# Seven heads' squares summed by one stationary column of ones into a row, read back as a column; attention logits kept negated

## The chip, the cores and the metric

The kernel runs on one core of one Trainium2 chip. The metric is the device time of one execution in microseconds (us); lower is better. Engines are named as in the profile: PE (TensorE, with PEld for its weight loads), DVE (VectorE), ACT (ScalarE), POOL (GpSimd) and SP (SyncE, which here only issues transfers).

## What is computed

One decoder layer over a sequence of 512 tokens, model width 1024, in float32. The part that the change touches is the differential attention: 8 heads, two softmaxes per head, the second one subtracted with a factor, and an RMS norm over the 128 values that a head gives for a token.

```python
def one_block(args):
    ...
    bias = jnp.transpose(bias_tab[rel_bucket(rel)], (2, 0, 1))
    logits = jnp.einsum('bqhcd,bkhcd->bhcqk', q_blk, k).astype(jnp.float32) * scale
    logits = logits + bias[None, :, None]
    logits = jnp.where(rel >= 0, logits, -jnp.inf)
    p = jax.nn.softmax(logits, axis=-1)
    attn = p[:, :, 0] - lam * p[:, :, 1]
    return jnp.einsum('bhqk,bkhe->bqhe', attn.astype(v.dtype), v)

out = lax.map(one_block, (qb, jnp.arange(nb, dtype=jnp.int32)))
out = jnp.transpose(out, (1, 0, 2, 3, 4)).reshape(B, S, N_HEADS, V_DIM)
out = rmsnorm(out, subln_g) * (1.0 - lambda_init)
```

Beside it run a recurrent branch (RG-LRU) and, after the merge of both, an MLP with squared ReLU.

## The kernel before

**Matmuls.** Each operand of a large matmul is split into a high part (fp32r, a cast on ACT) and a low part (the rest, a subtraction on DVE). `split` does both, `mm3` multiplies high by high, high by low and low by high into the same bank. Weights come through SP as raw tiles of 512 KB (`wraw`, two buffers), are split into `whi` and `wlo`, and feed the projections; a new load starts when DVE has made the low part out of the old raw tile.

**Attention as a pipeline of steps.** `attention` runs 32 steps: step s is head h = s // 4, block of 128 queries i = s % 4. What belongs to a step is spread over the following ones by `at(step, function)`:

- step s: `logits` (PE, two banks c = 0 and 1, width up to 512), then `soft_a`. It adds the bias table `toep` to the logits and takes each row's maximum (one DVE instruction per c, the profile's CUSTOM_DVE_ANT_0, and a short read of its accumulator), negates both maxima in one more instruction (`nm`), and ACT takes the exponential of logit minus maximum with a running sum.
- step s+1: `soft_b` (DVE) joins both softmaxes into `pe`.
- step s+2: `turn` transposes `pe` on PE; ACT casts the high part, and `turn_low` (DVE) makes the low part `pt`.
- step s+3, for every second block: `av` multiplies by the values. After a head's last block `post_a` copies the output (`of`) and squares it (`osq`) on ACT.

**The norm of a head** follows, counted from the head's last block s: at s+4 `post_b` sums the squares over the 128 partitions. For each of four token blocks the squares are the stationary operand and a column `ones` (fp32) moves: one column comes out, tokens on partitions. DVE adds the epsilon term (`se`, `ms`), POOL raises it to -1/2 and writes it to DRAM (`rdram`). At s+5 `post_c` reads it back, broadcast to all partitions (`rb`, issued by POOL), and at s+7 `post_d` multiplies `of` by it and splits the product into `aT`, the input of the output projection.

**What sets the order.** DVE, ACT and POOL run their instructions in the order in which the program records them. Within a step that is the list `order`; between steps, `fill_in` records projection work of the next pair of heads (`qkv_pair`, or `gate` after the last pair) for a given amount of PE time. PE's matmuls and SP's transfers are recorded without such a chain, and the tile framework places them at build time; on the chip each queue then runs in its fixed order. The PSUM banks of attention come from a ring of five (`at`), those of the projections from a ring of three (`acc`).

The tile `sum` (128 x 1024) in the pool `stg` is used after attention, by `weight_sums`. The tiles `apart` (128 x 16) and `apart2` (128 x 32) are allocated and not used.

Of the kernel before, what the change touches and what calls it, by code (L numbers as in the profile page):

```python
# [13 lines left out]
F32 = mybir.dt.float32  # L14
F32R = mybir.dt.float32r
I32 = mybir.dt.int32
AF = mybir.ActivationFunctionType
ALU = mybir.AluOpType
# [3 lines left out]
P = 128  # L22
S = 512
DM = 1024
NT = S // P
KT = DM // P
NH = 8
# [12 lines left out]
def tile_block(ctx: ExitStack, tc: tile.TileContext, x, w_in, w_rga, w_rgx, w_pa, w_pr, w_o,  # L40
               w_up, w_dn, rel_bias, smalls, lamv, onehot, out):
    nc = tc.nc

    cp = ctx.enter_context(tc.tile_pool(name="cp", bufs=1))
    dp = ctx.enter_context(tc.tile_pool(name="dp", bufs=1, space=bass.MemoryType.DRAM))
    wp = ctx.enter_context(tc.tile_pool(name="wp", bufs=3))
    hp = ctx.enter_context(tc.tile_pool(name="hp", bufs=1))
    sm = ctx.enter_context(tc.tile_pool(name="sm", bufs=4))
    sm.tile([P, 16], F32, name="apart", bufs=1)
    es_ps = ExitStack()  # L50

    def psum_pool(name):
# [24 lines left out]
    V, A, G, T = InOrder(nc.vector), InOrder(nc.scalar), InOrder(nc.gpsimd), nc.tensor  # L77
# [65 lines left out]
    def split(hi, lo, src, scale=None):  # L143
        if scale is None:
            A.copy(hi, src)
            V.tensor_tensor(out=lo, in0=src, in1=hi.bitcast(F32), op=ALU.subtract)
        else:
            A.activation(hi, src, AF.Copy, scale=scale)
            V.scalar_tensor_tensor(out=lo, in0=src, scalar=scale, in1=hi.bitcast(F32), op0=ALU.mult, op1=ALU.subtract)
# [59 lines left out]
    make_identity(nc, ident)  # L209
    ones = cp.tile([P, 1], F32, name="ones")  # L210
    G.memset(ones, 1.0)
    mhalf = cp.tile([P, 16], F32, name="mhalf")
    G.memset(mhalf, -0.5)

# [65 lines left out]
    stg = es_act.enter_context(tc.tile_pool(name="stg", bufs=1, side="right"))  # L280
    summed = [{p: dp.tile([P, 1024], F32, name=f"up{n}{p}") for p in ("M5", "M7", "M6", "M4")} for n in range(2, 8, 2)]

    def weight_sums(behind):
        t = stg.tile([P, 1024], F32, name="sum")
        G.tensor_copy(t[:, :1], behind[:, :1])
        for n in range(2, 8, 2):
            for blocks in (((0, None), (1, "M5"), (3, "M6"), (2, "M4")), ((1, None), (3, "M7"))):
                for b, p in blocks:
                    if p:
                        G.dma_start(t, w_up[n, b], accum_op=ALU.add)  # L290
                        G.dma_start(summed[n // 2 - 1][p], t)
                    else:
                        G.dma_start(t, w_up[n, b])
# [17 lines left out]
    with tc.tile_pool(name="p1", bufs=1) as p1:  # L311
# [28 lines left out]
        ps = [[psum("at"), psum("at")] for z in range(2)]  # L340
        for k0, k1 in pieces:
# [8 lines left out]
            for k in range(k0, k1):  # L350
                sq = ssq if k == 0 else p1.tile([P, S], F32, tag="sq", name="sq", bufs=2)
# [22 lines left out]
        rb = p1.tile([P, S], F32, name="rb")  # L374
# [31 lines left out]
    tdram = dp.tile([NH, TW], F32, name="tdram")  # L406
    trep = [dp.tile([1, P * TW], F32, name=f"trep{h}", tag=f"trep{h}") for h in range(NH)]
    rdram = dp.tile([NH, S], F32, name="rdram")

    es_at = ExitStack()  # L410
    wk = es_at.enter_context(tc.tile_pool(name="wk", bufs=1, reuse_waits="tile"))
    t2 = {n: wk.tile([P, 2], F32, name=n) for n in ("ls", "le")}
    t8 = [wk.tile([P, KT], F32, name=n) for n in ("ab", "e", "den", "s", "s2", "po", "tmp", "mxl")]
    wk.tile([P, 32], F32, name="apart2")
    halves = slice(0, 64), slice(64, P)
    toep = {}

# [163 lines left out]
    def attention(fills, qks, vs, pads):  # L581
        st = {}
# [15 lines left out]
        def soft_a(s):  # L598
            h, i = place(s)
            n = P * (i + 1)  # L600
            lg = st[s]
            mx = sm.tile([P, 2], F32, tag="mx", name="mx")
            pe = [work("pe") for _ in range(2)]
            for c in range(2):
                V.tensor_tensor_reduce(out=pe[c][:, :n], in0=lg[c][:, :n], in1=toep[h][:, 384 - P * i:512], scale=1.0,
                                       scalar=-3e38, op0=ALU.add, op1=ALU.max, accum_out=mx[:, c:c + 1])
            nm = sm.tile([P, 2], F32, tag="nm", name="nm")
            V.tensor_scalar(out=nm, in0=mx, scalar1=-1.0, scalar2=None, op0=ALU.mult)
            if i == 0:
                st["sums", h] = sm.tile([P, 2, NT], F32, tag="sums", name="sums", bufs=3)  # L610
            sums = st["sums", h]
            for c in range(2):
                A.activation(pe[c][:, :n], pe[c][:, :n], AF.Exp, bias=nm[:, c:c + 1], accum_out=sums[:, c, i:i + 1])
            st[s] = pe

        def soft_b(s):
# [39 lines left out]
        def post_a(h):  # L656
# [4 lines left out]
            A.activation(sq, o, AF.Square)  # L661
            st["of", h] = of, sq

        def post_b(h):
            of, sq = st["of", h]
            ps = psum("at")
            for t in range(NT):
                T.matmul(ps[:, t:t + 1], sq[:, t * P:(t + 1) * P], ones, start=True, stop=True)  # L668
            s0 = st["sums", h][:, 0, :]
            se = sm.tile([P, NT], F32, tag="se", name="se", bufs=1)  # L670
            V.scalar_tensor_tensor(out=se, in0=s0, scalar=EPS, in1=s0, op0=ALU.mult, op1=ALU.mult)
            ms = sm.tile([P, NT], F32, tag="ms", name="ms")
            V.scalar_tensor_tensor(out=ms, in0=ps[:, :NT], scalar=1.0 / P, in1=se, op0=ALU.mult, op1=ALU.add)
            rs = sm.tile([P, NT], F32, tag="rs4", name="rs4")
            G.tensor_tensor(out=rs, in0=ms, in1=mhalf[:, :NT], op=ALU.pow)
            G.dma_start(rdram[h, :].rearrange("(p t) -> p t", p=P), rs)

        def post_c(h):
            rb_ = wk.tile([P, S], F32, tag="rb", name="rb")
            G.dma_start(rb_, rdram[h:h + 1, :].broadcast_to([P, S]))  # L680
            st["rb", h] = rb_

        def post_d(h):
            of = st["of", h][0]
# [7 lines left out]
        def at(step, f, *a):  # L692
            acts.setdefault(step, []).append((f, a))

        for s in range(NH * NT):
            h, i = place(s)
            at(s, logits, s)
            at(s, soft_a, s)
            at(s + 1, soft_b, s)
            at(s + 2, turn, s)  # L700
            at(s + 2, turn_low, s)
            if i % 2 == 1:
                at(s + 3, av, s)
            if i == 3:
                at(s + 3, post_a, h)
                at(s + 4, post_b, h)
                at(s + 5, post_c, h)
                at(s + 7, post_d, h)
        for h in range(2, NH):
            at(NT * h - 3, toep_in, h)  # L710
        order = [toep_in, post_c, post_b, av, post_a, turn, logits, soft_a, soft_b, post_d, turn_low]
        for step in sorted(acts):
            j = step // (2 * NT)
            if step >= 37:
# [642 lines left out]
    last_of_chunk, pe, queue, seq = {}, None, {}, []  # L1357
# [56 lines left out]
    for kind, a, p, pairs in steps:  # L1414
        o = kind, a, p
        if kind == "pl":
            oc, kc = int(p[1]) % 2, int(p[1]) // 2
            for half in range(2):
                pe = task("PE", 2.73, plain_go(o, half), (pe, lows[o]))
# [4 lines left out]
            if p == "b3":  # L1424
                pe = task("PE", 0.46, norm_go, (pe, norm_split))
                seq.append("norm")
                turn = task("DVE", dve(512), lambda: V.tensor_scalar(out=r2, in0=banks["norm"], scalar1=1.0 / DM, scalar2=EPS, op0=ALU.mult, op1=ALU.add), (pe,))
# [19 lines left out]
        for u in (slice(0, 1), slice(1, 2)) if split_y else (slice(0, 2),):  # L1447
            key = (*b, u.start) if split_y else b
            pe = bank_task(key, 2.73 * len(pairs) / 4 * (u.stop - u.start) / 2 + 0.17 * (fresh and o in STEADY and u.start == 0), product_go(o, pairs, u, fresh), [pe, *after], fresh)
# [103 lines left out]
    for n in range(TRIES):  # L1553
        at = rng.uniform(-20.0, best)
# [53 lines left out]
```

## Time and profile before

| | |
|---|---|
| median of 3 runs | 840.35 us (839.96 to 840.93) |
| the profiled execution's own time | 840.35 us |
| its span (first to last instruction) | 838.6 us |
| busy PE, DVE, ACT, POOL | 832.1, 654.8, 478.9, 104.0 us |
| granted TensorE clock | 1.00 |
| attention steps (exponentials of step 0 to 31) | 81.8 to 268.5 us |
| weight casts in 75 to 285 us | 25, of 1.04 us each |

A row of the timeline gives start, duration, engine, line, operation, the tiles written and read, shapes, a count, and in brackets the idle time before it with what ended it. Several equal instructions in a row are merged into one row with their count; its duration is then that of the whole group. Matmuls overlap in the pipeline, so the time that one takes is read from its start to the start of the next. A row of the windows gives, for a stretch of time, its length and the busy time with the count of instructions of PE, PEld, DVE, ACT and POOL, then the clock, the share of the transfer engines and GB/s. A row of the waits gives who waited for whom: microseconds in total, times, longest. SPq is SP's queue of transfers. A row of the transfers gives the issuing queue, the count, the size of one and the median time from issue to landing.

### The profile page before, as it was taken

How to read it: one execution, taken by the hardware profiler on the slowest of the kernel's cores; microseconds unless marked ns; L12 is line 12 of the kernel's file. 1: busy time of each engine (PE TensorE's matmuls, PEld its weight loads, DVE VectorE, ACT ScalarE, POOL GpSimd, SP SyncE). 2: the span in 40 equal slices, each digit the busy share in tenths (PEclk: the TensorE clock that was granted, in tenths of full speed). 3: DMA queues.
4: the chain of work that ended last, by engine and by line, in shares of the span. 5: the costliest groups of instructions: out<-in, count | busy, mean ns of one | idle time of the engine just before them, and what ended most of it. 6: DMA issues, size and time to landing. Idle time of an engine off the chain costs nothing.

```text
span 838.6 us, 14384 instructions
## 1 busy us (share of the span) xinstructions
PE 832.1 (99%) x5686; PEld 765.0 (91%) x5686; DVE 654.8 (78%) x1077; ACT 478.9 (57%) x753; POOL 104.0 (12%) x132
## 2 busy tenths in 40 slices
PE   9999999999999999999999999999999999999998
PEld 7899999999988887888888888899999999999998
DVE  6776788887877336879766767899989969977996
ACT  7445466555665334685763345774488448645851
POOL 0041231413201101111111000000000000000000
PEclk9999999999999999999999999999999999999999
DMA  6357332433322346667657662355655576556563
GB/s 202 124 153 217 91 110 66 103 123 91 88 77 76 88 138 196 195 189 209 182 170 179 197 253 76 101 151 145 209 151 151 151 256 170 144 164 200 151 168 110
DMA packets 41172, 126.10 MB, mean 150 GB/s; under 512 B 4992, under 2 KB 9800, under 8 KB 41104
## 3 DMA queue, kind: packets, MB, share of 16 engines
q1 hardware_dynamic: 31152, 92.65, 33.6%
q0 software_dynamic: 9952, 32.53, 18.1%
q8 instruction: 45, 0.74, 0.3%
q14 instruction: 23, 0.19, 0.1%
HBM read 102.05 MB, written 11.05 MB: 135 GB/s over the span
## 4 chain that ended last, share of the span: by engine, by line
PE 87%; DVE 5%; DMA 4%; ACT 2%; issue 1%; SPq 0%; ACTq 0%; DVEq 0%
PE acc L69 37%; PE acc L139 14%; PE acc L140 13%; PE acc L141 13%; DMA wraw<-in_w_in_dram 3%; PE at L595 2%; DVE wlo L69 2%; PE at L139 2%; PE at L141 2%; PE at L140 2%; PE at L631 1%; ACT whi L69 1%; PE at L529 1%; DVE pe L69 1%; PE at L668 1%
## 5 line engine op out<-in xcount | busy, mean ns | idle before, releaser
L69 ACT CAST whi<-raw 128x1024 fp32r<-128x1024 f32 x109 | 112.2, 1049 | 93.8 <-DVE raw L69 34.1
L69 DVE TENSOR_TENSOR wlo<-wraw,whi 128x1024 fp32r<-128x1024 f32 (+2 forms) x86 | 96.9, 1148 | 73.7 <-ACT whi L69 73.6
L69 PE MATMUL acc<-us,whi 128*128 128x256 f32 x900 | 153.8, 277 | 0.0
L69 PE MATMUL acc<-h,whi 128*128 128x256 f32 (+1 forms) x851 | 153.7, 285 | 0.0
L69 DVE TENSOR_TENSOR wlo<-raw,whi 128x1024 fp32r<-128x1024 f32 x109 | 131.0, 1218 | 21.0 <-ACT whi L69 20.9
L69 PEld LDWEIGHTS acc<-us,whi 128*128 128x128 f32 x900 | 135.8, 188 | 0.0
L69 PEld LDWEIGHTS acc<-h,whi 128*128 128x128 f32 x851 | 130.7, 188 | 2.6
L69 PE MATMUL acc<-us,wlo 128*128 128x256 f32 x448 | 123.8, 276 | 0.0
L69 PE MATMUL acc<-h,wlo 128*128 128x256 f32 (+1 forms) x424 | 120.6, 285 | 0.0
L69 ACT CAST whi<-wraw 128x1024 fp32r<-128x1024 f32 (+2 forms) x86 | 82.5, 982 | 47.1 <-DMA wraw<-in_w_in_dram 31.6
L139 PE MATMUL acc<-whi,hT 128*128 128x256 f32 x384 | 108.3, 282 | 0.0
L140 PE MATMUL acc<-wlo,hT 128*128 128x256 f32 x384 | 107.1, 279 | 0.2 <-DVE wlo L69 0.2
L69 PEld LDWEIGHTS acc<-us,wlo 128*128 128x128 f32 x448 | 84.1, 188 | 0.0
L139 PE MATMUL acc<-hT,whi 128*128 128x512 f32 x208 | 81.7, 393 | 0.0
L141 PE MATMUL acc<-hT,wlo 128*128 128x512 f32 x208 | 81.2, 390 | 0.0
L69 PEld LDWEIGHTS acc<-h,wlo 128*128 128x128 f32 x424 | 79.6, 188 | 1.3
L141 PE MATMUL acc<-whi,hT 128*128 128x256 f32 x288 | 80.1, 278 | 0.0
L69 ACT ACTIVATE pe<-pe,nm 128x128 f32<-128x128 f32 (+3 forms) x64 | 35.6, 558 | 66.0 <-DVE nm L69 66.0
L140 PEld LDWEIGHTS acc<-wlo,hT 128*128 128x128 f32 x384 | 72.4, 188 | 0.6 <-DVE wlo L69 0.4
L139 PEld LDWEIGHTS acc<-whi,hT 128*128 128x128 f32 x384 | 72.3, 188 | 0.5 <-issue 0.2
L69 POOL TENSOR_TENSOR rs<-ms,mhalf 128x8 f32<-128x8 f32 (+1 forms) x25 | 39.4, 1579 | 187.2 <-DVE ms L69 187.2
L69 POOL DMA_DIRECT2D raw<-raw x24 | 20.7, 863 | 325.7 <-DVE raw L69 117.2
(208 smaller groups left out, 1749.0 us busy)
## 6 DMA issues: line engine op xcount, KB each, us to landing
wraw<-in_w_in_dram SPq DMA_DIRECT2D x54, 512.0 KB, 3.5
raw<-in_w_dn_dram SPq DMA_DIRECT2D x32, 512.0 KB, 4.3
raw<-in_w_up_dram SPq DMA_DIRECT2D x29, 512.0 KB, 4.3
raw<-raw POOLq DMA_DIRECT2D x24, 512.0 KB, 4.6
sum<-in_w_up_dram POOLq DMA_DIRECT2D x18, 512.0 KB, 5.5
wraw<-in_w_pa_dram SPq DMA_DIRECT2D x8, 512.0 KB, 4.7
wraw<-in_w_pr_dram SPq DMA_DIRECT2D x8, 512.0 KB, 4.3
wraw<-in_w_o_dram SPq DMA_DIRECT2D x8, 512.0 KB, 4.2
```

The lines of the kernel that those rows point to most:

```text
L69: ins = f(*a, **k)
L139: T.matmul(o, l[0], r[0], start=first, stop=False)
L140: T.matmul(o, l[0], r[1], start=False, stop=False)
L141: T.matmul(o, l[1], r[0], start=False, stop=last)
L529: T.transpose(out=ps[:, t * P:(t + 1) * P], in_=qn[t // 2][:, c0:c0 + P], identity=ident)
L595: T.matmul(lg[c][:, :N], qT[:, c, i * P:(i + 1) * P], qk[h % 2, z][:, c, :N], start=z == 1, stop=z == 2)
L631: T.transpose(out=tp[:, b * P:(b + 1) * P], in_=st[s][:, b * P:(b + 1) * P], identity=ident)
L668: T.matmul(ps[:, t:t + 1], sq[:, t * P:(t + 1) * P], ones, start=True, stop=True)
```

## The change

Two things are changed.

**Sums of squares.** For heads 0 to 6 the squares are split in two fp32r parts (`post_p`, step s+3, into the tile `sum`). `post_b` (s+4) makes a column of ones the stationary operand and moves both parts, 512 tokens each, into one bank: a row of 512 sums on one partition. `post_e` copies the row to SBUF (ACT) and writes it to DRAM (`mdram`, a transfer issued by ACT). `post_l` (s+5) reads it back through SP as a column per token block (`few`, which the profile names apart2 or apart). `post_c` (s+6) now holds the epsilon term, the power and the store to `rdram`; `post_r` (s+7) reads the broadcast, for these heads through SP; `post_d` comes one step later, at s+8. Head 7 keeps the old form and its steps. In `order`, `post_b` moves from before `av` to behind `logits`.

**Negated logits.** `soft_a` lets the DVE instruction scale by -1 and take the minimum, so that the accumulator is the negated maximum at once; the exponential scales by -1. The separate negation of the maxima is gone, and `nm` has eight buffers.

```diff
-    sm.tile([P, 16], F32, name="apart", bufs=1)
+    ones_r = sm.tile([P, 16], F32R, name="apart", bufs=1)[:, :1]
...
+    G.memset(ones_r.bitcast(F32), 1.0)
...
-    wk.tile([P, 32], F32, name="apart2")
+    few = wk.tile([P, 2, 4, NT], F32, name="apart2")
...
-            mx = sm.tile([P, 2], F32, tag="mx", name="mx")
+            nm = sm.tile([P, 2], F32, tag="nm", name="nm", bufs=8)
...
-                V.tensor_tensor_reduce(out=pe[c][:, :n], in0=lg[c][:, :n], in1=toep[h][:, 384 - P * i:512], scale=1.0,
-                                       scalar=-3e38, op0=ALU.add, op1=ALU.max, accum_out=mx[:, c:c + 1])
-            nm = sm.tile([P, 2], F32, tag="nm", name="nm")
-            V.tensor_scalar(out=nm, in0=mx, scalar1=-1.0, scalar2=None, op0=ALU.mult)
+                V.tensor_tensor_reduce(out=pe[c][:, :n], in0=lg[c][:, :n], in1=toep[h][:, 384 - P * i:512], scale=-1.0,
+                                       scalar=3e38, op0=ALU.add, op1=ALU.min, accum_out=nm[:, c:c + 1])
...
-                A.activation(pe[c][:, :n], pe[c][:, :n], AF.Exp, bias=nm[:, c:c + 1], accum_out=sums[:, c, i:i + 1])
+                A.activation(pe[c][:, :n], pe[c][:, :n], AF.Exp, scale=-1.0, bias=nm[:, c:c + 1], accum_out=sums[:, c, i:i + 1])
...
+        def post_p(h):
+            if h == NH - 1:
+                return
+            of, sq = st["of", h]
+            both = stg.tile([P, 2, S], F32R, tag="sum", name="osr")
+            split(both[:, 0], both[:, 1], sq)
+            st["of", h] = of, both
+
         def post_b(h):
-            of, sq = st["of", h]
+            both = st["of", h][1]
             ps = psum("at")
-            for t in range(NT):
-                T.matmul(ps[:, t:t + 1], sq[:, t * P:(t + 1) * P], ones, start=True, stop=True)
-            s0 = st["sums", h][:, 0, :]
+            if h == NH - 1:
+                for t in range(NT):
+                    T.matmul(ps[:, t:t + 1], both[:, t * P:(t + 1) * P], ones, start=True, stop=True)
+                st["ms", h] = ps[:, :NT]
+                post_c(h)
+                return
+            for z in range(2):
+                T.matmul(ps[:1, :], ones_r, both[:, z], start=z == 0, stop=z == 1)
+            st["row", h] = ps
+
+        def post_e(h):
+            if h == NH - 1:
+                return
+            ps = st["row", h]
+            row = wk.tile([P, S], F32, tag="osq", name="row")[:1, :]
+            A.copy(row, ps[:1, :])
+            A.dma_start(mdram[h:h + 1, :], row)
+
+        def post_l(h):
+            ms = st["ms", h] = few[:, h % 2, 0, :]
+            nc.sync.dma_start(ms, mdram[h, :].rearrange("(t p) -> p t", p=P))
+
+        def post_c(h):
+            s0, got = st["sums", h][:, 0, :], st["ms", h]
...
-            V.scalar_tensor_tensor(out=ms, in0=ps[:, :NT], scalar=1.0 / P, in1=se, op0=ALU.mult, op1=ALU.add)
+            V.scalar_tensor_tensor(out=ms, in0=got, scalar=1.0 / P, in1=se, op0=ALU.mult, op1=ALU.add)
...
-        def post_c(h):
-            rb_ = wk.tile([P, S], F32, tag="rb", name="rb")
-            G.dma_start(rb_, rdram[h:h + 1, :].broadcast_to([P, S]))
-            st["rb", h] = rb_
+        def post_r(h):
+            rb_ = st["rb", h] = wk.tile([P, S], F32, tag="rb", name="rb")
+            (G if h == NH - 1 else nc.sync).dma_start(rb_, rdram[h:h + 1, :].broadcast_to([P, S]))
...
                 at(s + 3, post_a, h)
+                at(s + 3, post_p, h)
                 at(s + 4, post_b, h)
-                at(s + 5, post_c, h)
-                at(s + 7, post_d, h)
+                at(s + 4, post_e, h)
+                if h < NH - 1:
+                    at(s + 5, post_l, h)
+                    at(s + 6, post_c, h)
+                    at(s + 7, post_r, h)
+                    at(s + 8, post_d, h)
+                else:
+                    at(s + 5, post_r, h)
+                    at(s + 7, post_d, h)
...
-        order = [toep_in, post_c, post_b, av, post_a, turn, logits, soft_a, soft_b, post_d, turn_low]
+        order = [toep_in, post_l, post_c, post_r, av, post_a, turn, logits, post_b, soft_a, soft_b, post_p, post_e, post_d, turn_low]
```

How this moves instructions is shown at three places, all around head 0's sum of squares. PE first, before the change: ten rows of one step behind the last product with the values. `acc` are projections, `ones,osq` is the sum of squares.

```order
L595 MATMUL at<-kl_487,qkT 128x384
L139 MATMUL acc<-whi,hT 128x256
L140 MATMUL acc<-wlo,hT 128x256
L141 MATMUL acc<-whi,tail 128x256
L139 MATMUL acc<-whi,hT 128x256
L140 MATMUL acc<-wlo,hT 128x256
L141 MATMUL acc<-whi,tail 128x256
L139 MATMUL acc<-whi,hT 128x256
L668 MATMUL at<-ones,osq 128x1 x4
L140 MATMUL acc<-wlo,hT 128x256
```

The sum stands 7 projection matmuls behind the logits of step 6; another 20 projection matmuls follow, and then the transposes (`ident,pe`) and the logits of step 7. PE after the change, at the end of the same stretch (`osr,apart` are the two new matmuls, apart being the ones):

```order
L139 MATMUL acc<-whi,hT 128x256
L631 MATMUL at<-ident,pe 128x128 x2
L597 MATMUL at<-qkT 128x512
L597 MATMUL at<-kl_489,qkT 128x512
L597 MATMUL at<-qkT 128x512
L597 MATMUL at<-kl_489,qkT 128x512
L682 MATMUL at<-osr,apart 1x512 x2
L140 MATMUL acc<-wlo,hT 128x256
```

Between the logits of step 6 and the transposes there are now 26 projection matmuls and no sum of squares; the sum stands behind the logits of step 7. In heads 2 and 4 the new order has the same 26.

DVE in step 6 before the change (ISA rows are the addition with row maximum and the read of its accumulator; `wlo` are weights):

```order
L69 ISA pe,mx<-at,toep 128x384
L69 ISA mx 128x1
L69 ISA pe,mx<-at,toep 128x384
L69 ISA mx 128x1
L69 TENSOR_SCALAR nm<-mx 128x2
L69 RECIPROCAL rc<-sums 128x1
L69 SCALAR_TENSOR_TENSOR r_1428<-sums,lneg,rc 128x1
L69 SCALAR_TENSOR_TENSOR pe<-pe,r_1428 128x256
L69 TENSOR_TENSOR pt_496<-at,pt_495 128x128
```

And after it:

```order
L69 ISA pe,nm<-at,toep 128x384
L69 ISA nm 128x1
L69 ISA pe,nm<-at,toep 128x384
L69 ISA nm 128x1
L69 RECIPROCAL rc<-sums 128x1
L69 SCALAR_TENSOR_TENSOR r_1416<-sums,lneg,rc 128x1
L69 SCALAR_TENSOR_TENSOR pe<-pe,r_1416 128x256
L69 TENSOR_TENSOR osr<-osq,osr 128x512
L69 TENSOR_TENSOR pt_498<-at,pt_497 128x128
```

The negation is gone, and the low part of the squares stands between `pe` and the low part of the transposed block. `se` and `ms`, which stood in step 7, stand in step 9, ahead of its two additions; `ms` there reads the column.

ACT after the change, steps 6 and 7 of the same head (`whi` are weights, `v` the values, `qkT` queries):

```order
L69 COPY of<-at 128x512
L69 ACTIVATE osq<-at 128x512
L69 CAST pt_497<-at 128x128
L69 ACTIVATE pe,sums<-pe,nm 128x384 x2
L69 CAST osr<-osq 128x512
L69 CAST whi<-wraw 128x1024 x2
L69 CAST v<-acc 128x512
L69 CAST pt_497<-at 128x2x128
L69 ACTIVATE pe,sums<-pe,nm 128x512 x2
L69 COPY row<-at 1x512
L69 DMA mdram<-row 1x512
L69 ACTIVATE qkT<-at,qg 64x512 x2
```

The rows osr, row and mdram are new; the others stood in this order before. Each of the two exponentials of a step now waits for its own accumulator read, where before the first waited for the negation of both.

On SP, each of the seven heads adds a read of the column and a read of the broadcast between the weight loads; on POOL seven of the eight broadcast reads are gone.

More of the change, by code (lines that the diff above doesn't have):

```diff
@@ L283, in weight_sums @@
     def weight_sums(behind):
-        t = stg.tile([P, 1024], F32, name="sum")
+        t = stg.tile([P, 1024], F32, tag="sum", name="sum")
         G.tensor_copy(t[:, :1], behind[:, :1])
@@ L408, in tile_block @@
     rdram = dp.tile([NH, S], F32, name="rdram")
+    mdram = dp.tile([NH, S], F32, name="mdram")
     es_at = ExitStack()
```

## Prediction

> **What bounds the kernel now.** I read the page first, then the windows, then what TensorE (PE) waits for, then single rows in order of time.
>
> ```profile
> span 838.6 us, 14384 instructions
> ...
> PE 832.1 (99%) x5686; PEld 765.0 (91%) x5686; DVE 654.8 (78%) x1077; ACT 478.9 (57%) x753; POOL 104.0 (12%) x132
> ```
>
> PE shows 99%, but a busy PE need not be a fast one. So here is a stretch of the attention part, 75 to 295 us, and every wait of PE in it:
>
> ```profile
> 200.00:220.00 20.00, 19.68 (x161) 18.99 (x161) 16.68 (x47) 13.02 (x30) 6.61 (x8) 1.00 0.31 82
> ...
> PE at L631 <- DVE pe L69: 0.3, 1, 0.3
> ...
> PEld at L631 <- issue: 1.0, 3, 0.4
> PEld at L631 <- DVE pe L69: 0.6, 3, 0.2
> ```
>
> The granted clock is 1.00. DVE (VectorE) has 3.3 us of 20 left in that stretch, ACT 7. In 220 us PE itself waits once, for 0.3 us, and its weight loads for a few tenths each. The attention part is therefore bound by PE's instruction stream: what is taken out of that stream shortens the span, as long as no other engine is then late. What stands behind attention is PE work too, so a gain there is not waited away later.
>
> **What the change takes from PE.** Today each head's squares cost eight PE passes (four matmuls of one column in fp32, two passes each). Head 4 and head 0:
>
> ```profile
> 214.02 0.28 PE L141 MATMUL acc<-whi,tail 128*128 128x256 f32 x1
> 214.14 0.95 PE L668 MATMUL at<-ones,osq 128*128 128x1 f32 x8
> 214.94 0.36 PE L139 MATMUL acc<-whi,hT 128*128 128x256 f32 x1
> 215.14 0.28 PE L140 MATMUL acc<-wlo,hT 128*128 128x256 f32 x1
> ...
> 114.20 0.28 PE L139 MATMUL acc<-whi,hT 128*128 128x256 f32 x1
> 114.49 1.05 PE L668 MATMUL at<-ones,osq 128*128 128x1 f32 x8
> 115.40 0.36 PE L140 MATMUL acc<-wlo,hT 128*128 128x256 f32 x1
> 115.60 0.28 PE L141 MATMUL acc<-whi,hT 128*128 128x256 f32 x1
> ```
>
> I go by starts, since durations of pipelined matmuls overlap. A 256-column matmul takes 0.12 (214.02 to 214.14). From 214.14 to 215.14 are 1.00 us, of which one such matmul is 0.12: the group costs 0.88, its slow change back to the other kind of matmul included. In head 0, which also waits for the squares, 114.20 to 115.60 less two matmuls is 1.16. Six heads at 0.88 and head 0 at 1.16 make 6.4 us.
>
> In their place come two fp32r matmuls of 512 columns for each of the seven heads, with one stationary column. The nearest rows are the MLP norm's pair, also ones against 512 fp32r columns, but with 128 stationary columns, and a matmul with few stationary columns, in fp32:
>
> ```profile
> 55.25 1.26 PE L452 MATMUL at<-oh,rbt 64*32 64x512 f32 x4
> ...
> 546.61 0.62 PE L69 MATMUL acc<-s,h 128*128 128x512 f32 x2
> 547.07 0.39 PE L69 MATMUL acc<-h,whi 128*128 128x256 f32 x2
> ```
>
> The norm's pair takes 0.46 (546.61 to 547.07). The other row moves 2 x (512+128) = 1280 columns in 1.26, or 1.0 us for 2 x 512. I take 0.46, because type and size are those of the norm's pair; the ends are 0.46 and 1.0. Seven pairs are 3.2 us, so PE's stream gets **3.2 us shorter** (6.4 - 3.2). The Trainium skill, "TensorE: Matmul & The Clock Gate", section "Back-to-back issue gap", makes the time one of moving columns alone (N/2.4 + 2.5 ns): two at 512 would be an estimated 0.43, and seven 3.0. No row here shows it for one stationary column.
>
> **What PE then waits for.** The removed group stood in front of the next pair of transposes and of the logits of the step after; the new pair stands behind those logits. So PE reaches both sooner, and their inputs must be ready sooner. Head 0:
>
> ```profile
> 113.50 0.28 PE L139 MATMUL acc<-whi,hT 128*128 128x256 f32 x1
> ...
> 117.76 0.38 PE L631 MATMUL at<-ident,pe 128*128 128x128 f32 x2
> ...
> 118.91 0.28 PE L139 MATMUL acc<-whi,hT 128*128 128x256 f32 x1
> ...
> 115.38 0.08 DVE L69 DVE_READ_ACCUMULATOR2_ANT mx<- 128x1 f32 x1
> ...
> 115.97 0.17 DVE L69 TENSOR_SCALAR nm<-mx 128x2 f32<-128x2 f32 x1
> 116.05 0.15 DVE L69 RECIPROCAL rc<-sums 128x1 f32<-128x1 f32 x1
> ...
> 116.50 0.48 DVE L69 SCALAR_TENSOR_TENSOR pe<-pe,r 128x256 f32<-128x256 f32 x1
> ...
> 116.18 0.62 ACT L69 ACTIVATE pe<-pe,nm 128x384 f32<-128x384 f32 x1 [1.59 <-DVE nm L69]
> ...
> 117.39 1.98 ACT L69 CAST whi<-wraw 128x1024 fp32r<-128x1024 f32 x2
> ```
>
> The new order has 26 projection matmuls between the logits and the transposes: from 113.50 at 0.114 each PE arrives at 116.46 instead of 117.76. What it transposes, pe, is finished at 116.98, or 116.90 without the negation (only 0.08 later than nm does rc start). PE waits 0.45 there. From the transposes to the end of the logits are 1.15 us (117.76 to 118.91), so the new pair is reached at 118.05.
>
> Is its input there by then? The negation goes, and with it the one wait of both exponentials on nm: each waits only for its own row minimum. The first may start once the first read is done, 115.46 and a hop of 0.04 (nm ends at 116.14, the exponential starts at 116.18), so at 115.50. Both take 1.21 (116.18 to 117.39), so ACT is free for the new cast at 116.71, and DVE's subtraction follows it:
>
> ```profile
> L69 ACT CAST s<-scratch x1: 622/622/622, 532.0 to 532.0; 128x512 fp32r<-128x512 f32 x1
> L69 DVE TENSOR_TENSOR s<-scratch,s x1: 684/684/684, 533.0 to 533.0; 128x512 fp32r<-128x512 f32 x1
> ```
>
> 116.71 + 0.62 + 0.68 = 118.01. The first matmul needs only the cast half, the second starts 0.23 later: no second wait. With the exponentials where they are today the cast would start at 117.39 and the subtraction end at 118.69, a further 0.4 behind the second matmul's 118.28.
>
> Heads 2 and 4 stand in the same order, 26 matmuls, so I count 0.45 three times: **1.4 us back**. In heads 1, 3, 5 and 6 more work lies between the logits and the new pair, or the pe in question is ready sooner; I take nothing, and keep 0 to 0.45 for each.
>
> **What is added beside PE.** DVE loses 32 negations at 0.08 and gains seven subtractions at 0.68: 4.8 against 2.6, and while it waits for the cast it does nothing. The product with rb and the second subtraction of each head move one step later, out of the step that gets the new one, so that step is no longer than today. ACT gains the cast (0.62), the row's copy and a DMA issue per head (rows of 0.59 and 0.38 stand further down), into its waits:
>
> ```profile
> ACT pe L69 <- DVE nm L69: 66.0, 29, 3.7
> ...
> SPq L103 <- DVE wlo L69: 148.0, 22, 17.2
> ```
>
> 66 us of ACT's idle time cover seven times about 1.6. The 14 transfers that SP's queue gets stand among weight loads that wait 148 us for raw buffers already; in this part ACT has no wait for a weight, so a few microseconds of delay there cost nothing. Without that cover each would push back a cast and what follows on ACT. POOL loses seven issues; it is 12% busy. I put these together at -0.2: the existing waits for pe shrink a little. Range -0.8 to +1.
>
> **Sum**: -3.2 + 1.4 - 0.2 = -2.0 us. The profiled execution took 840.35 with a span of 838.6 (1.75 lies around it), and 840.35 is the median of the runs too. Forecast: span 836.6, time **838.3**.
>
> **Rivals.** *DVE takes it back.* DVE has 3.3 us of 20 left. If heads 1, 3 and 5 wait 0.45 as well, another 1.35 goes and the time is 839.7; with the second wait of 0.4 in three heads, 840.9. For it: heads 0 to 5 run in the same dense part. Against: DVE's own list does not get longer in the crowded step.
>
> *One stationary column is no cheaper than the row with 32.* At 1.0 a pair, seven cost 7.0: -3.2 becomes +0.6, and the sum 842.1. Against: that row is fp32.
>
> *The column comes late, and the kernel is slower.* The sum now goes PSUM, row, DRAM, column, and DVE's ms waits for it in order. Decisive is head 6, where the low half of the last transposed block stands behind ms, and the last product of attention (av) behind that:
>
> ```profile
> 268.37 0.18 ACT L69 ACTIVATION_READ_ACCUMULATOR pe<-pe,nm 128x1 f32 x1
> ...
> 274.79 0.69 DVE L69 TENSOR_TENSOR pt<-at,pt 128x512 fp32r<-128x512 f32 x1
> ...
> 278.41 0.59 ACT L69 COPY of<-at 128x512 f32<-128x512 f32 x1 [3.65 <-PE at L141]
> ...
> 0.74 0.38 SPq L325
> ...
> rdram<-rs POOLq DMA_DIRECT2D x8, 2.0 KB, 2.3
> ...
> rbt<-in_rel_bias_dram SPq DMA_DIRECT2D x1, 1.0 KB, 3.2
> ...
> xT<-in_x_dram SPq DMA_DIRECT2D x3, 512.0 KB, 7.3
> ```
>
> From the exponentials (268.55, or 0.7 sooner, 267.85): copy 0.59, issue 0.38, landing 2.3, issue 0.38, so the read starts at 271.5. It must be in by 274.7 to change nothing: 3.2 us. Those products end at 278.4 and take twelve matmuls, 1.4, so they begin at 277.0 and there is about 1.5 more before PE waits: it decides from a read of **4.7 us** on. No row shows a read of 512 single elements; the nearest by size take 2.3 to 3.2, the slowest of all 7.3. I take 3.2. At 7.3 head 6 costs 2.6. Heads 1, 3 and 5, with shorter steps, I estimate at 1 each, so 5.6 in all: 843.9, slower. The Trainium skill speaks against the change here: "DMA: Bandwidth & Descriptors", section "Rules for kernel authors", says that a last dimension that isn't contiguous becomes one descriptor per element, here 512 of 4 bytes. By that rule the late case comes true if such descriptors run much slower than the 16-byte pieces of rdram<-rs, whose 128 landed in 2.3.
>
> *It gains more.* With no wait at the transposes and fewer of today's: -3.2 - 1.2, so 836.0.
>
> **How the numbers follow.** Forecast 0.50 (its own range 837.0 to 839.6), DVE takes it back 0.22, the column late 0.12, the dear column 0.06, more gain 0.10. The range 836.2 to 842.1 leaves out most of the late column and half of the larger gain. Some 0.2%, or 1.7 us, is what a measurement of this kernel tells from no change. Faster by more than that: the larger gain and 0.43 of the forecast, 0.53. Within: the rest of the forecast and nearly all of the give-back, 0.30. Slower: the late column, most of the dear one, 0.17.
>
> **What would show it.** The new pair's starts 0.23 apart, and 0.46 to the next matmul; exponentials that start 0.65 sooner after their logits; PE waits of 0.3 to 0.6 before the two transposes of heads 0, 2 and 4, on DVE's pe; no DVE wait before ms of over 1 us, and none of PE before the last av. I am wrong if the pair takes 1.0, if PE waits for osr, or if DVE stands at ms for several microseconds.

## The result, and the profile after

The changed kernel takes **837.9 us** (median of 22 runs, 835.85 to 840.8) against 840.2 for the kernel before (22 runs): ratio 0.9972, 95% interval 0.9963 to 0.9981. The forecast was 838.3. The time came out as predicted, but by luck: two errors cancel, as the experiments show. The execution that was profiled took 836.11 us, 1.8 below its own median, so differences in its trace are read by mechanism and not added up to the result.

The page of the changed kernel, span and busy time:

```profile
span 834.3 us, 14347 instructions
...
PE 828.1 (99%) x5644; PEld 759.1 (91%) x5644; DVE 654.2 (78%) x1052; ACT 486.0 (58%) x767; POOL 99.8 (12%) x126
```

PE has 42 matmul records fewer (seven times eight passes against two). DVE is as busy as before, because the subtractions (7 x 0.69) cost about what the negations saved (32 x 0.17); ACT has 7 us more.

Now step 6 of the changed kernel, the part in which head 0's squares are prepared (timeline, rows of ACT, DVE and PE):

```profile
113.35 0.56 DVE L69 CUSTOM_DVE_ANT_0 pe<-at,toep 128x384 f32<-128x384 f32 x1
...
113.97 0.62 ACT L69 ACTIVATE pe<-pe,nm 128x384 f32<-128x384 f32 x1
...
114.76 0.48 DVE L69 SCALAR_TENSOR_TENSOR pe<-pe,r 128x256 f32<-128x256 f32 x1
...
115.18 0.60 ACT L69 CAST osr<-osq 128x512 fp32r<-128x512 f32 x1
...
115.82 0.69 DVE L69 TENSOR_TENSOR osr<-osq,osr 128x512 fp32r<-128x512 f32 x1 [0.58 <-ACT osr L69]
115.82 0.38 PE L631 MATMUL at<-ident,pe 128*128 128x128 f32 x2
...
116.97 0.62 PE L682 MATMUL at<-osr,apart 128*1 128x512 f32 x2
117.43 0.28 PE L140 MATMUL acc<-wlo,hT 128*128 128x256 f32 x1
```

The pair costs 0.46 (116.97 to 117.43), as forecast. Here `pe` is ready at 115.24, and the transposes at 115.82 wait for nothing. DVE stands 0.58 for the cast of the squares.

Without the negation two things come sooner, counted from the step's first reduction. In the kernel before, that reduction started here:

```profile
114.89 0.56 DVE L69 CUSTOM_DVE_ANT_0 pe<-at,toep 128x384 f32<-128x384 f32 x1
```

With the two rows of step 6 in the prediction, the first exponential started 1.29 later (116.18), and now 0.62; DVE's own join, which writes the `pe` that PE transposes, started 1.61 later (116.50), and now 1.41. The join comes some 0.2 sooner in most of the 32 steps.

What PE and its weight loads wait for from 75 to 295 us in the changed kernel (us in total, times, longest):

```profile
PE at L631 <- DVE pe L69: 0.4, 2, 0.2
PE acc L141 <- DVE wlo L69: 0.3, 1, 0.3
...
PEld at L631 <- DVE pe L69: 1.3, 4, 0.4
PEld acc L141 <- DVE wlo L69: 0.7, 1, 0.7
PEld at L139 <- ACT pt L69: 0.7, 3, 0.3
PEld at L631 <- issue: 0.6, 3, 0.3
PEld at L597 <- issue: 0.5, 2, 0.3
PEld at L631 <- ACT pe L69: 0.5, 2, 0.2
PEld acc L139 <- issue: 0.5, 3, 0.2
```

With two more rows of 0.2 these are 5.9 us. The same list of the kernel before has, beside the three rows that the prediction shows, these five, and adds up to 3.8:

```profile
PEld at L139 <- ACT pt L69: 0.5, 2, 0.3
PEld at L529 <- DVE qn L69: 0.5, 2, 0.3
PEld at L595 <- issue: 0.5, 2, 0.3
PEld at L668 <- ACT osq L69: 0.2, 1, 0.2
PEld at L140 <- DVE pt L69: 0.2, 1, 0.2
```

None of these rows is large, but their sum matters for this case: 3.8 before, 5.9 after, and from 0.2 to 22.3 in the experiments below. A held-up load and the matmul behind it both have rows, so the sum is not exact. Nor does it rank kernels with different streams: the changed kernel waits more than the kernel before and is faster.

### The profile page after: what moved, and what is told of

Read it like the earlier page. It is cut to its first block, busy times and chain, and to the rows that moved or that the text cites. A ratio compares the mean times of both kernels' runs of the same rounds, so it can differ in the third digit from the quotient of the medians.

```text
span 834.3 us, 14347 instructions
## 1 busy us (share of the span) xinstructions
PE 828.1 (99%) x5644; PEld 759.1 (91%) x5644; DVE 654.2 (78%) x1052; ACT 486.0 (58%) x767; POOL 99.8 (12%) x126
## 2 busy tenths in 40 slices
DMA packets 45329, 126.11 MB, mean 151 GB/s; under 512 B 8695, under 2 KB 13503, under 8 KB 45262
## 4 chain that ended last, share of the span: by engine, by line
PE 90%; DVE 4%; ACT 2%; DMA 2%; issue 1%; SPq 0%; POOL 0%; DVEq 0%; ACTq 0%; POOLq 0%
PE acc L69 37%; PE acc L141 15%; PE acc L140 15%; PE acc L139 15%; PE at L597 2%; PE at L139 2%; PE at L141 2%; PE at L140 2%; DVE wlo L69 2%; PE at L631 1%; DMA wraw<-in_w_in_dram 1%; PE at L531 1%; DVE pe L69 1%; ACT pe L69 0%; DVE xT L69 0%
## 5 line engine op out<-in xcount | busy, mean ns | idle before, releaser
L69 ACT CAST whi<-wraw 128x1024 fp32r<-128x1024 f32 (+2 forms) x86 | 82.6, 982 | 43.7 <-DMA wraw<-in_w_in_dram 29.2
L139 PE MATMUL acc<-hT,whi 128*128 128x512 f32 x208 | 81.5, 392 | 0.0
L69 ACT ACTIVATE pe<-pe,nm 128x128 f32<-128x128 f32 (+3 forms) x64 | 35.6, 559 | 43.9 <-DVE nm L69 43.7
L140 PE MATMUL acc<-hT,whi 128*128 128x512 f32 x156 | 60.8, 390 | 0.0
```

Of the source, the lines that this page charges most:

```text
L69: ins = f(*a, **k)
L139: T.matmul(o, l[0], r[0], start=first, stop=False)
L140: T.matmul(o, l[0], r[1], start=False, stop=False)
```

## The experiments

### The two edits apart

**Only the negated logits**, on the kernel before:

```diff
-            mx = sm.tile([P, 2], F32, tag="mx", name="mx")
+            nm = sm.tile([P, 2], F32, tag="nm", name="nm", bufs=8)
...
-                                       scalar=-3e38, op0=ALU.add, op1=ALU.max, accum_out=mx[:, c:c + 1])
-            nm = sm.tile([P, 2], F32, tag="nm", name="nm")
-            V.tensor_scalar(out=nm, in0=mx, scalar1=-1.0, scalar2=None, op0=ALU.mult)
+                                       scalar=3e38, op0=ALU.add, op1=ALU.min, accum_out=nm[:, c:c + 1])
...
-                A.activation(pe[c][:, :n], pe[c][:, :n], AF.Exp, bias=nm[:, c:c + 1], accum_out=sums[:, c, i:i + 1])
+                A.activation(pe[c][:, :n], pe[c][:, :n], AF.Exp, scale=-1.0, bias=nm[:, c:c + 1], accum_out=sums[:, c, i:i + 1])
```

> The kernel before with only the logits' edit: the reduction writes the negated logits and their minimum, the exponential takes scale -1, the 32 negations of the maximum on DVE are gone; the squares are summed as before. Theory (the gain of 2.3 us is the shorter matmul stream, PE being the bound): 839.5 to 840.2 us, ratio 0.9993 to 1.0000, because each exponential starts some 0.6 us sooner but PE waits for none of them. Rival (the sooner exponentials are the gain): 838 us, ratio 0.997. In the trace the first waits for nm on ACT should shrink in both cases (ACT's pe <- DVE nm summed 66.0 us over 29 waits before and 43.7 over 26 after, from 75 to 295 us).

Measured: 837.23 us, ratio 0.9963 (0.9949 to 0.9977). My theory fell. The negation alone gives as much as the whole change.

**Only the new sums**: the changed kernel with the old maximum and its negation put back (the same lines the other way round).

> The changed kernel with the logits' edit undone: maximum of the plain logits, then a negation of its own on DVE; the sums of squares, their row, the way through DRAM and the order as after. Theory: the stream is 3.1 us shorter as after, but the exponentials start some 0.6 us later, so osr's low half comes up to 0.4 us late at the pair in heads 0, 2 and 4 and the transposes' waits grow: 838.2 to 839.4 us, ratio 0.9976 to 0.9990. Rival (the gain needs the negation): 840 us or more. Second rival (the negation is without any effect): 837.9, ratio 0.9972.

Measured: 847.34 us, ratio 1.0083 (1.0062 to 1.0104), 7 us slower than before and far behind the theory (838.2 to 839.4); the first rival, 840 or more, came true. The sums, meant to relieve PE, are a loss by themselves.

**Only the place of the sum**, behind the logits, on the kernel before:

```diff
-        order = [toep_in, post_c, post_b, av, post_a, turn, logits, soft_a, soft_b, post_d, turn_low]
+        order = [toep_in, post_c, av, post_a, turn, logits, post_b, soft_a, soft_b, post_d, turn_low]
```

> The kernel before with one name moved in the order of a step: the sums of squares (the old four matmuls of plain float32 with a column of ones, and the two small DVE operations behind them) stand behind the logits rather than ahead of them. Theory (order matters only by what PE waits for, and PE waited for nothing there): 839.9 to 840.6 us, ratio 0.9995 to 1.0005. Rival (the place behind the logits is a gain of its own, since the logits and so the exponentials start 0.88 us sooner): 839 us or less. Other rival (DVE stands at ms for the later sums and holds up the softmax behind it): 841 or more.

Measured: 840.49 us, ratio 1.0001 (0.9985 to 1.0017), as the theory had it.

**No return through DRAM**, the changed kernel without these two transfers:

```diff
-            A.dma_start(mdram[h:h + 1, :], row)
...
-            nc.sync.dma_start(ms, mdram[h, :].rearrange("(t p) -> p t", p=P))
```

> The changed kernel without the two transfers of the return: the row is still copied out of PSUM, but it isn't written to DRAM and no column is read; the mean squares of seven heads are taken as 1.0 from a tile set once, so the computation leaves out that the sums reach the normalisation. Theory (the column lay ready 2.4 to 7 us ahead of its use, the issues stand on queues off the path): 837.7 to 838.2 us, the time after, ratio to before 0.9969 to 0.9976. Rival (the return costs something by ACT's issues of 0.2 us or the 512 packets of 4 bytes): 836.5 to 837.3.

Measured: 840.27 us, ratio 0.9999 (0.9986 to 1.0011): less work, and 2.4 us slower than the changed kernel. No theory had that. Its waits name something the missing transfers have no part in, the low part of the transposed block ahead of `av`:

```profile
PE at L140 <- DVE pt L69: 1.9, 4, 0.7
...
PEld at L140 <- DVE pt L69: 2.9, 4, 0.9
```

The order of its matmuls, in turn, differs from the changed kernel's: by the names of their operands, 442 of the 5644 PE instructions in the two traces differ from those at the same place. The framework places PE's matmuls and SP's transfers at build time, and any edit makes it place them anew. So an edit and the order that it happens to get had to be separated.

### The same edits with PE's order held

The next kernels record each matmul and each transfer of SP and tie it to the one ahead of it in a given list, so that both queues run in an order chosen by me:

```diff
+    for u, v in zip(place_PE, place_PE[1:]):
+        tc.add_manual_dep(issued['PE'][v], issued['PE'][u].name, ORDER, reason="order")
```

and the same for SP. The added recorder has line 90, which the profile then shows for every matmul. The traces have PE's instructions in exactly the given order. The complete changed kernel was not run with its own order held; the nearest to it is the kernel without the return, below.

**Negated logits, in the order of the kernel before:**

> The kernel before with only the logits negated, but its matmuls and SP's transfers held in the order in which they stand in the kernel before (each depends on the one ahead of it, so the builder cannot place them anew). Two theories for the 3.1 us that the negation alone gained in the free build (837.23 against 840.31): A, the builder's new order of the matmuls (51 starts that are 60 to 120 ns late between 75 and 345 us where before has 74, since the sums of squares now stand beside the transposes; 6.6 to 4.5 us), with which the time here stays at 839.3 to 840.3; B, the exponentials that start sooner on the chip, with which it is 837.0 to 838.3 here too.

Measured: 836.99 us, ratio 0.9953 (0.9936 to 0.9970). Theory B: the gain is on the chip and not in the placing. Of all the waits of PE and its loads from 75 to 295 us one row is left:

```profile
PEld at L90 <- ACT osq L69: 0.2, 1, 0.2
```

3.8 us became 0.2: without the negation PE waits for almost nothing. Whether the sooner exponentials do that, as the expectation has it, or DVE's sooner join is not shown, since the edit brings both. One row of the kernel before, in the same stretch, speaks for the join: the join of a step (it begins with `rc`) had to wait for exponentials once, for 0.3.

```profile
DVE rc L69 <- ACT pe L69: 0.3, 1, 0.3
```

**The kernel before, in the order of the kernel with negated logits:**

> The kernel before, instruction for instruction, but its matmuls and SP's transfers held in the order in which the builder placed those of the kernel with only the logits negated. Theory A (the order is the gain): 837.3 to 838.8, the 2.1 us of fewer late starts being there without the negation. Theory B (the sooner exponentials are): the transposes stand too early for the old softmax, PE waits for pe by up to 0.65 in many of 32 steps, 841 us or more.

Measured: 846.72 us, ratio 1.0069 (1.0054 to 1.0085). Theory B again: this order gives nothing to the kernel that has the negation, and is 5.5 us slower for it than its own (841.23 in that session). The waits come to 15.4. These are the ones for the softmax, where the former kernel has none, and loads that the profile puts down to no one (`issue`); another 4.1 are for DVE's `qkT`:

```profile
PE at L90 <- DVE pe L69: 3.4, 6, 1.2
...
PEld at L90 <- issue: 4.1, 5, 1.4
PEld at L90 <- DVE pe L69: 2.1, 5, 0.7
```

**No return, in the order of the changed kernel:**

> The changed kernel without the row's write to DRAM and the column's read (the seven heads' mean squares are taken as 1.0, the row is copied but not used), with the matmuls and SP's other transfers held in the order of the changed kernel. If the 840.27 of the free build without the return came from its new order of the matmuls, this is 837.4 to 838.2, the time after, as the column lay ready 2.4 us or more ahead. If the column's read holds up something that no wait shows, 836.0 to 837.3. If leaving it out is slower on the chip itself (a transfer that comes sooner and is in the way), 839.5 or more.

Measured: 838.22 us, ratio 0.9964 (0.9953 to 0.9976), the changed kernel's time within the intervals, and at the edge of the first expectation. So the return costs nothing that can be measured, and the 840.27 came from the placing.

**The new sums without the negation, in the order of the changed kernel:**

> The changed kernel with the plain logits, their maximum and the 32 negations of it on DVE put back, matmuls and SP's transfers held in the order of the changed kernel. The free build took 847.34. If it was the placing of its matmuls that cost most (the pair of sums torn apart, late starts of 0.3 to 3 us), this is 839 to 842: exponentials 0.65 us later, so PE waits longer at transposes where it waited already and up to 0.4 at the sums of heads 0, 2 and 4. If the softmax with the new work on ACT and DVE is the bound by itself, 845 or more in this order too.

Measured: 848.27 us, ratio 1.0084 (1.0068 to 1.0100), the second expectation: the softmax with the new work is the bound, in this order too. All rows of PE's waits add up to 22.3 us; among the largest are these:

```profile
PE at L90 <- DVE pe L69: 3.5, 9, 0.5
...
PEld at L90 <- DVE pe L69: 4.2, 10, 0.7
PEld at L90 <- ACT row L69: 2.7, 5, 0.8
PEld at L90 <- DVE osr L69: 1.9, 3, 0.6
```

And head 0 in its timeline, the place shown above:

```profile
116.80 0.48 DVE L69 SCALAR_TENSOR_TENSOR pe<-pe,r 128x256 f32<-128x256 f32 x1
...
117.43 0.41 PE L90 MATMUL at<-ident,pe 128*128 128x128 f32 x2 [0.46 <-DVE pe L69]
```

A wait of this size is what the prediction expected in the changed kernel (0.45). There `pe` is ready at 115.24, 0.58 before PE comes for it, and the wait is missing. The late low half of the squares, which the prediction priced at 0.4 in three heads for exponentials that stay where they are, is here too (`osr`, three waits).

### What takes the sums' gain back

**The changed kernel without the pair of matmuls:**

```diff
-            for z in range(2):
-                T.matmul(ps[:1, :], ones_r, both[:, z], start=z == 0, stop=z == 1)
-            st["row", h] = ps
+            st["row", h] = both[:, 0].bitcast(F32)
```

> The changed kernel without the pair of matmuls in heads 0 to 6 (the row is taken from the first partition of the rounded squares, so the sums over partitions are left out); everything else, the cast and the subtraction too, in the order of the changed kernel. Theory from the runs so far: the changed kernel waits in PE's stream for the softmax that the split of the squares holds up on ACT and DVE (late starts over 30 ns make 9.1 us between 75 and 345 us against 5.5 in the kernel before with negated logits and its own order). Then 7 x 0.46 = 3.2 us less stream bring less than 2: 836.2 to 837.5. Rival, the prediction's view that PE's stream is the bound: 834.7, the full 3.2.

Measured: 837.82 us, ratio 0.9964 (0.9951 to 0.9977). Taking 3.2 us out of PE's stream brings **nothing** that can be measured, less even than the 0.4 to 1.7 of the expectation. What was taken out comes back as waits (5.9 before the edit, 8.6 now):

```profile
PE at L90 <- DVE pe L69: 1.5, 3, 0.6
...
PEld at L90 <- DVE pe L69: 2.4, 4, 0.8
PEld at L90 <- issue: 1.3, 6, 0.3
PEld at L90 <- DVE qn L69: 1.0, 2, 0.5
```

In the changed kernel PE's stream is therefore not the bound in attention; what PE then waits for is mostly DVE's results (`pe`, `qn`).

**One rounded pass instead of the split**, in the same order: ACT's square writes fp32r, and cast, subtraction and one matmul of each pair go.

```diff
-            split(both[:, 0], both[:, 1], sq)
...
-            for z in range(2):
-                T.matmul(ps[:1, :], ones_r, both[:, z], start=z == 0, stop=z == 1)
+            T.matmul(ps[:1, :], ones_r, both, start=True, stop=True)
```

> The changed kernel with squares that ACT writes rounded to fp32r at once: no cast (0.62 on ACT), no subtraction and no wait for the cast (0.68 + 0.96 on DVE) per head, one matmul in place of the pair; the sums leave out the low part of the squares. Matmuls and SP's transfers in the order of the changed kernel. If the split on ACT and DVE is what gave the stream's gain back: 1.6 us of stream and 2 to 3.5 us of late starts go, 833 to 834.5. If the split costs nothing and only the matmul counts: 836.3.

Measured: 834.63 us, ratio 0.9930 (0.9907 to 0.9953), the fastest of all: 3.3 us less than the changed kernel, and 3.2 less than the run before it, where removing both matmuls had brought nothing. So the cast on ACT and the subtraction on DVE are what takes the sums' gain back. They account for 1.7 to 3.3 us: without them the stream counts again, and up to 1.6 of the gain may be the one matmul per head that goes with them. All rows of waits add up to 2.7, and of those for `pe` one is left:

```profile
PEld at L90 <- DVE pe L69: 0.2, 1, 0.2
```

The traces place these gains in attention. The first matmul of the output projection (`aT`) starts at 300.87 in the kernel before, 298.09 in the changed one, 297.32 with the logits negated and the old order held, 298.14 without the pair and 293.33 here. From there to the end of the span it is 536.3 to 539.6 in all 14 traces, so the traces differ by up to 3 us behind attention too.

**The same one pass, placed by the builder:**

> The changed kernel with squares that ACT writes rounded to fp32r at once, as in the run held in the changed kernel's order (the sums leave out the squares' low part), but placed by the builder. Expected within 1 us of the held one, 833 to 835.5, and so faster than both kernels, if the split of the squares on ACT and DVE gave the gain back; 836.3 if only the matmul counts.

Measured: 838.12 us, ratio 0.9966 (0.9952 to 0.9980), 3.5 us more than the same instructions in the held order. I had expected at most 1. The waits for `pe`, 0.2 in all when held, are back:

```profile
PE at L631 <- DVE pe L69: 0.7, 3, 0.3
...
PEld at L631 <- DVE pe L69: 1.5, 4, 0.5
```

**The subtraction one step later**, the whole computation, placed by the builder:

```diff
-            split(both[:, 0], both[:, 1], sq)
+            A.copy(both[:, 0], sq)
...
+        def post_q(h):
+            both, sq = st["lo", h]
+            V.tensor_tensor(out=both[:, 1], in0=sq, in1=both[:, 0].bitcast(F32), op=ALU.subtract)
...
+                    at(s + 4, post_q, h)
...
-        order = [toep_in, post_l, post_c, post_r, av, post_a, turn, logits, post_b, soft_a, soft_b, post_p, post_e, post_d, turn_low]
+        order = [toep_in, post_l, post_c, post_r, av, post_a, turn, logits, post_q, post_b, soft_a, soft_b, post_p, post_e, post_d, turn_low]
```

> The changed kernel, complete, with the subtraction for the low part of the squares moved on DVE from behind the join of step s+3 to the start of step s+4, ahead of its logits' reductions, so that DVE no longer stands 0.96 us per head for the cast (6.7 us over seven heads). The builder places the matmuls. If that standing is the cost: 835 to 836.5. If the 0.68 of the subtraction itself is, in either place, or the cast on ACT: 837.5 to 838.5.

Measured: 838.7 us, ratio 0.9983 (0.9969 to 0.9997), nearest to the second expectation. DVE hardly stands for the cast any more (0.4 in all, where it was 6.7), yet nothing is gained, and PE now waits at the pair:

```profile
PE at L687 <- DVE osr L69: 0.5, 2, 0.3
...
PEld at L687 <- DVE osr L69: 1.2, 3, 0.5
```

Since the builder's order alone was worth 3.5 us in the run before it, this one doesn't settle how much of the split's price is DVE's standing, how much the subtraction and how much ACT's cast.

## Why the prediction was right, and where it was wrong

The time was right. The reason given for it was not. By the prediction the sums carried the gain (-3.2 of stream, +1.4 of waits), and the negation was worth a part of -0.2, beside keeping the low half of the squares in time. By the runs the negation is the gain (-3.1 by itself: 837.23 placed anew, 836.99 in the old order), and the sums add nothing to it: 837.9 for both is 0.7 to 0.9 more, by the ratios 0.8 to 1.6, and the intervals overlap. The two errors, some 3 us each, cancel, and that is luck.

1. **What bounds the kernel: the step that failed.** "The attention part is therefore bound by PE's instruction stream: what is taken out of that stream shortens the span, as long as no other engine is then late." In the changed kernel the condition did not hold, and the rows above that sentence could have shown it: they had PE and its loads waiting "a few tenths each" and were not added up. Added up with their neighbours they were 3.8 us, more than the change was to bring. Stream and softmax were in balance within a few microseconds. Making the softmax shorter removed the waits and gave 3.1 to 4 us (ratios 0.9963 and 0.9953); making the stream shorter, once the split had made the softmax longer, gave none (the run without the pair). Stream and waits have to be taken together. With the prediction's 6.4 for the old groups and the 0.46 of a pair, an estimate of both against the kernel before gives -2.1 for the one pass held, 0.2 for the negated logits held, 2.2 without the pair, 2.7 for the changed kernel, 3.8 before, 15.4 for the kernel before in the other order and 19.1 for the sums without the negation held; the times of these seven stand in the same order. Of the kernels placed anew two fall out of it, the one pass (0.8) and the one without the return (7.8).
2. **The stream's term, -3.2.** Right in itself: pairs of 0.46, starts 0.23 apart. The estimate of 0.43 for a pair by the Trainium skill ("TensorE: Matmul & The Clock Gate", "Back-to-back issue gap") is 0.03 below the 0.46 measured. That section gives the formula for a matmul by itself; no run here shows the 131 ns that it gives at 512 columns for a stream of loads and matmuls. One stationary column was no cheaper and no dearer than the 128 of the norm's pair, 0.46 as well.
3. **The waits before transposes, +1.4.** Too large. In head 0 there is none, and in heads 2 and 4 half of it (0.35 and 0.34 between the starts where 0.11 is usual). Head 2:

```profile
163.28 0.28 PE L141 MATMUL acc<-whi,hT 128*128 128x256 f32 x1
163.63 0.41 PE L631 MATMUL at<-ident,pe 128*128 128x128 f32 x2
```

   I had left DVE's work at its old times relative to PE while PE moved.
4. **The rest, -0.2.** Mis-sized on both sides. "The existing waits for pe shrink a little" was, without the split, a matter of nearly all of PE's waits, 3.8 to 0.2. One cause may be the price of a negation: by the prediction 0.08, the distance from `nm` to `rc`, while the join starts 0.20 sooner without it (1.61 to 1.41). And "DVE's own list does not get longer in the crowded step" left out the time that DVE stands for the cast, which the prediction named and did not price. Two rows of the changed kernel's waits:

```profile
ACT pe L69 <- DVE nm L69: 43.7, 26, 2.5
...
DVE osr L69 <- ACT osr L69: 6.7, 7, 1.5
```

   The cover that I had named for ACT's new work did shrink (66.0 to 43.7). DVE's standing of 6.7 us, seven times 0.96, comes on top of 4.8 us of subtractions; how much of it PE feels is open (the run with the later subtraction).
5. **The rivals.** *DVE takes it back* comes nearest to what the runs show for the sums, and was priced too low, at 1.35 to 2.6: without the negation the sums cost 7 us. The shares of DVE and of ACT's cast in it were not separated. *The dear column* and *the late column* did not come. The column was read in time in every head; the list of transfers has the median from issue to landing, and the timeline head 6, which the prediction called decisive:

```profile
apart<-mdram SPq DMA_DIRECT2D x7, 2.0 KB, 2.1
```

```profile
264.01 0.38 SPq L695 DMA_DIRECT2D apart<-mdram  x1
...
271.49 0.16 DVE L69 SCALAR_TENSOR_TENSOR ms<-apart,se 128x4 f32<-128x4 f32 x1
```

   Issued at 264.01 and in after a median of 2.1, it had over 5 us to spare. The prediction had the issue at 271.5, on the old times of the exponentials. One of its signs of being wrong did come, and not by the column: in head 7, which keeps the old form, DVE stands 6.13 at `ms` (0.89 before).

```profile
278.44 0.16 DVE L69 SCALAR_TENSOR_TENSOR ms<-at,se 128x4 f32<-128x4 f32 x1 [6.13 <-PE at L677]
```

   The one pass in the held order has this wait of 6.1 too, and is the fastest kernel. The rule of the Trainium skill that spoke against the change ("DMA: Bandwidth & Descriptors", "Rules for kernel authors") did not decide here: 512 pieces of 4 bytes land as soon as the 2.0 KB of rdram, 2.1 us too. (The trace has 8695 packets under 512 bytes, that of the kernel without the return 4992, some 529 fewer for each of the seven columns.)

What stays open: whether the sooner exponentials or DVE's sooner join give the negation's gain, how the placing that the builder found for the changed kernel compares with the best one for it, and the shares of cast, subtraction, standing and the second matmul in the 3.3 us.

## What to carry to other kernels

When an engine shows 99% busy, add up all its small waits, those of its weight loads too, before calling its stream the bound: if the sum is of the size of the gain that is hoped for, two chains may be in balance, and shortening the one while lengthening the other gave nothing here. Where a framework orders instructions at build time, an experiment should hold that order, since the builder's new placing alone was worth 2 to 3.5 us here, and an order made for another kernel 5.5; both can hide what an edit does. Work that relieves one engine by a dependent pair on two others has to be priced there too: the cast and the subtraction took back 1.7 to 3.3 us.

## What the runs showed of the hardware

- Loading one stationary column in fp32r takes less than half of the time that 128 columns take; both rows are of the changed kernel, a group (least, median and longest in ns) and a line of the timeline:

```profile
L682 PEld LDWEIGHTS at<-osr,apart x14: 81/82/83, 116.7 to 260.4; 128*1 128x1 f32 x14
```

```profile
297.87 0.19 PEld L139 LDWEIGHTS acc<-aT,whi 128*128 128x128 f32 x1
```

- The issue of the row's store took ACT 0.20 us in six of the seven heads (0.47 in the first), the issue of the column's read took SP 0.38 (above). The two transfers differ in shape as well as in queue, so which of these makes the difference is not shown:

```profile
L69 ACTq DMA_DIRECT2D mdram<-row x7: 200/201/475, 123.0 to 262.9; - x7
```
